# Gaps of 64 and 128 bytes ahead of the weight buffers of a two-layer encoder on one core

## The chip, the core and the metric

The kernel runs on one core of a Trainium2 chip. TensorE multiplies, VectorE, ScalarE and GpSimd work beside it on the same on-chip memory (SBUF, 128 partitions), DMA queues bring weights from HBM. The metric is the device time of one execution in microseconds. The kernel before took 1790.79 us (median of three runs, 1790.58 to 1791.91).

## The reference

The input is x with 512 tokens of 1024 features, in float32. There are two layers; each does

```python
x = x + 0.5 * swiglu(rms_norm(x, ffn1_norm[l]), ffn1_w_gate[l], ffn1_w_up[l], ffn1_w_down[l])
h = rms_norm(x, mix_norm[l])
p = h @ w_in[l]                       # latents of q and kv, rotary key, conv columns
attn = mla_group(...)                 # 8 heads, block-causal in chunks of 64
conv = conv_group(...)                # gate, causal depthwise conv of 31 taps, LayerNorm, silu
x = x + concatenate([attn, conv]) @ w_out[l]
x = x + 0.5 * swiglu(rms_norm(x, ffn2_norm[l]), ffn2_w_gate[l], ffn2_w_up[l], ffn2_w_down[l])
x = rms_norm(x, post_norm[l])
```

with `swiglu(x, g, u, d) = (silu(x @ g) * (x @ u)) @ d` and an inner width of 2816. Nearly all arithmetic is in the four feed-forward blocks.

## The kernel before

Features stand on the partitions and the 512 tokens along the free axis, so a tile of 128 features is 2048 bytes a partition. A product in float32 is made of three matmuls in a reduced float32 format (FR in the code): each operand is split into a high part, the operand rounded to FR, and a low part, what is left. `mm3` (lines 169 to 173) issues the three for one block of 128 x 128 weights: high weights with the high half of the moving operand (L170), the same weights with its low half (L171), low weights with its high half (L172). The moving operand has 512 columns, or 256 where a block works on half the tokens. `load_w` (lines 147 to 159) brings weights by a DMA of SyncE into a raw tile; ScalarE casts it to the high part (L151) and VectorE subtracts to the low part (L157). `split_into` (lines 257 to 263) does the same from tiles that are there already (L260, L262).

The feed-forward block of one layer (`ffn_body`) goes through the inner width in four chunks. The first pairs of columns are plain products. In the others, `pair` and `down` use a scheme with seven products in place of eight, on sums and differences of quarters of the weights and of x; most of these products have a moving operand of 256 columns. In some (`product_joined`, L389 and L390) the moving tile xj holds the high and the low half side by side: L389 multiplies all 512 columns by the high weights, L390 the first 256 by the low weights. The mixer (`mix_body`) has the same `mm3` for its projections; in `latent_k`, `queries` and `up_kv` the weights are the moving operand and the activations the stationary one.

The order of the work is the order in which the code issues it, with a scheduler of the framework behind it and some `issue_after` constraints that name an instruction by hand. Each engine works its own list and waits by semaphores.

The tiles lie in SBUF pool after pool, in the order in which the pools are opened, and inside a pool tag after tag, in the order of a tag's first use. The pools are: constants and x; the ring of 35 tiles of 2048 bytes (r), from which nearly all split activations come; 5 temporary tiles (t); the weights' pool with 3 raw buffers, 4 high (wh) and 4 low (wl) of 4096 bytes; a pool of small tiles; and then, by turns, the pool of a feed-forward block (fr raw quarters, xj and xs moving tiles, ls low weights that a DMA with addition makes) or that of the mixer (m and others). A pool that is larger by some bytes moves all that lies behind it.

What an address is for the change is the offset of a buffer's first byte in a partition. All large buffers have multiples of 512 bytes, so one offset modulo 512 holds for a whole tag. In the kernel before, ring, temporary, raw, wh and wl tiles are at 192, and fr, xj, xs, ls and m at 224.

Of the kernel before, what the change touches and what calls it, by code (L numbers as in the profile page):

```python
# [7 lines left out]
FP = mybir.dt.float32  # L8
FR = mybir.dt.float32r
# [6 lines left out]
P = 128  # L16
# [4 lines left out]
NT = S // P  # L21
H = 8
DN = 64
DR = 32
# [7 lines left out]
NF = F // P  # L32
EPS = 1e-6
WC = 1024
HS = S // 2
RING = 35
WIDE = 6
# [41 lines left out]
def encoder_kernel(ctx: ExitStack, tc: tile.TileContext, xT, consts, vecs, rgain, wgu1, wd1, wdq1,  # L79
# [6 lines left out]
    wpool = ctx.enter_context(tc.tile_pool(name="w", bufs=4))  # L86
    small = ctx.enter_context(tc.tile_pool(name="small", bufs=2))
# [3 lines left out]
    def nm(s):  # L91
        uid[0] += 1
        return f"{s}{uid[0]}"

    def slot(dt=FP, w=S):
        return ring.tile([P, w], dt, tag="r", name=nm("r"))
# [4 lines left out]
    def bank():  # L101
        return psum.tile([P, S], FP, tag="ps", name=nm("ps"))
# [10 lines left out]
    def tiny(tag, w, dt=FP):  # L113
        return small.tile([P, w], dt, tag=tag, name=nm(tag))

    V, A, G, T = nc.vector, nc.scalar, nc.gpsimd, nc.tensor

    x = cpool.tile([P, KD, S], FP, name="x")
# [28 lines left out]
    def load_w(src, w, kind=""):  # L147
        raw = wpool.tile([P, WC], FP, tag="raw", name=nm("raw"), bufs=3)
        nc.sync.dma_start(out=raw[:, :w], in_=src)
        hi = wpool.tile([P, WC], FR, tag="wh", name=nm("wh"))  # L150
        order["cast"] = A.copy(hi[:, :w], raw[:, :w]).ins  # L151
        lo = low()
        if kind == "sum":
            A.activation(lo[:, :w], raw[:, :w], AF.Copy, scale=-1.0)
            G.dma_start(out=lo[:, :w], in_=src, accum_op=ALU.add)
            return hi, lo
        (G if kind in POOLW.split() else V).tensor_tensor(lo[:, :w], raw[:, :w], hi[:, :w].bitcast(FP),  # L157
                                                          ALU.subtract)
        return hi, lo

    def low():
        return wpool.tile([P, WC], FR, tag="wl", name=nm("wl"))

# [5 lines left out]
    def mm3(o, lh, ll, rh, rl, first, last, free=False):  # L169
        T.matmul(o, lh, rh, start=first, stop=False, skip_group_check=free)  # L170
        T.matmul(o, lh, rl, start=False, stop=False, skip_group_check=free)  # L171
        order["mm"] = T.matmul(o, ll, rh, start=False, stop=last, skip_group_check=free).ins  # L172
        return order["mm"]
# [74 lines left out]
    def groups(srcs, rhs, ws=None):  # L248

        ws = ws or [load_w(src, WC) for src in srcs]  # L250
        os = [bank() for _ in srcs]
# [4 lines left out]

    def split_into(q, src, w=WC):

        hi = wpool.tile([P, WC], FR, tag="wh", name=nm("wh"))
        A.copy(hi[:, :w], src[:, :w])  # L260
        lo = low()
        order["lo"] = V.tensor_tensor(lo[:, :w], src[:, :w], hi[:, :w].bitcast(FP), ALU.subtract).ins  # L262
        return hi, lo
# [5 lines left out]
    def ffn_body(fpool, l, gx, norm, wgu, wd, wdq, gain, done, w0, halved):  # L269
# [52 lines left out]
        def operands(R):  # L322

            def joined(src):
                both = fpool.tile([P, 2, S], FR, tag="xj", name=nm("xj"), bufs=WIDE)
                A.copy(both[:, :, 0:HS], src)
                V.tensor_tensor(both[:, :, HS:S], src, both[:, :, 0:HS].bitcast(FP), ALU.subtract)
                return both
# [13 lines left out]
            for i in range(2):  # L342
                e, o = wide(quarter()), wide(quarter())
                for j in range(2):
                    for par, t in ((0, e), (1, o)):
                        m = 4 * i + 2 * j + par
                        V.scalar_tensor_tensor(t[:, j], x[:, m, :], gain[:, m:m + 1], R, ALU.mult, ALU.mult)
                        yield
                b11, b12, b21, b22 = (v[:, :, h * HS:(h + 1) * HS] for v in (e, o) for h in range(2))
                for n, src in (("b11", b11), ("b21", b21)):  # L350
# [21 lines left out]
        def product(o, w, n, start, stop):  # L372
            with tc.issue_after(order["pe"]):
                for gu in range(2):
                    for k in range(4):
                        hi, lo = X[n][k // 2]
                        t = slice(k % 2 * HS, (k % 2 + 1) * HS)
                        c = slice(gu * 512 + k * P, gu * 512 + (k + 1) * P)
                        last = mm3(o[:, gu * HS:(gu + 1) * HS], w[0][:, c], w[1][:, c], hi[:, t], lo[:, t],
                                   start and gu == 0 and k == 0, stop and k == 3, True)  # L380
            order["pe"] = last

        def product_joined(os, w, n, start):
            with tc.issue_after(order["pe"]):
                for gu, o in enumerate(os):
                    for k in range(4):
                        both = X[n][k // 2][:, k % 2]
                        c = slice(gu * 512 + k * P, gu * 512 + (k + 1) * P)
                        T.matmul(o, w[0][:, c], both, start=start and k == 0, stop=False, skip_group_check=True)  # L389
                        last = T.matmul(o[:, 0:HS], w[1][:, c], both[:, 0:HS], start=False, stop=k == 3,  # L390
                                        skip_group_check=True).ins
# [237 lines left out]
    def mix(l, gx, norm, done):  # L629
        with tc.tile_pool(name="k", bufs=4) as kpool:  # L630
            mix_body(kpool, l, gx, norm, done)

    def mix_body(kpool, l, gx, norm, done):
# [49 lines left out]
        cqT, ckT, pq, scqs, vs = [], [], [], [], []  # L683
        ssl, sspe = tiny("ssl", NT), tiny("sspe", NT)
        ckl = [slot().rearrange("p (t c) -> p t c", t=2) for _ in range(NT // 2)]
        cke = tiny("cke", NT * DR).rearrange("p (t d) -> p t d", t=NT)
        q = kpool.tile([P, NT, H, DQ], FP, tag="q", name=nm("q"), bufs=1)
        kn = kpool.tile([P, NT, H, DQ], FP, tag="kn", name=nm("kn"), bufs=1)
        cq, wkl_, sk, ckc, ratio = (tiny(n, NT) for n in ("cq", "wkl", "sk", "ckc", "ratio"))
# [346 lines left out]
    class Finish:  # L1036
# [54 lines left out]
        def __call__(self):  # L1091
# [4 lines left out]
            for t in range(NT):  # L1096
# [8 lines left out]
    st = Stats()  # L1105
    f = gained(0, "g1", gx, first_gain)
    f(0)
    w0 = [tuple(wpool.tile([P, WC], t, tag=tag, name=nm(tag), bufs=n)
                for t, tag, n in ((FP, "raw", 3), (FR, "wh", 4), (FR, "wl", 4))) for _ in range(2)]

    def half_w(q, gu):
        raw, hi, lo = (v[:, gu * 512:(gu + 1) * 512] for v in w0[q])
# [12 lines left out]
    w0 = [w[1:] for w in w0]  # L1125
# [172 lines left out]
```

## Time and profile before

| What | Value |
|---|---|
| median of three runs | 1790.79 us |
| profiled execution, its own time | 1792.67 us |
| its span, first to last instruction | 1790.6 us |
| TensorE busy, of the span | 99% |
| weight loads busy | 88% |
| VectorE, ScalarE, GpSimd busy | 83%, 61%, 21% |
| granted TensorE clock | 0.999 |
| mean HBM traffic | 127 GB/s |

The three runs lie within 0.1% of each other. The page calls TensorE's matmuls PE and its weight loads PEld; a weight load is a row of its own beside the matmuls. Matmuls are pipelined, so the busy time of a group is the union of durations that overlap, and the spacing of matmuls is read from the starts in the timeline. A row of the groups gives the line, the engine, the tile written and those read (buffer numbers left out), the shapes, the count, busy time, mean duration of one, and idle time before.

### The profile page before, as it was taken

The page shows a single profiled execution, that of the slowest core. Times are in us where ns is not written, and L with a number is a line of the kernel's source. Part 1 is how long each engine was busy: PE and PEld are TensorE (multiplying, and loading weights), DVE is VectorE, ACT ScalarE, POOL GpSimd, SP SyncE. Part 2 cuts the span into 40 slices and gives each one's busy share as a digit, 9 for nine tenths or more (in the row PEclk, how much of TensorE's full clock was granted, in tenths as well). Part 3 has the DMA queues.
Part 4 walks back from the last instruction along what each step waited for, and adds up shares of the span by engine and source line. Part 5 has one row for each costly group of instructions (what it writes and reads, how often), then busy time and mean ns, then how long its engine had stood idle before and what let it go on. Part 6 is the DMA issues. An engine that isn't in the chain of part 4 may idle for free.

```text
span 1790.6 us, 29441 instructions
## 1 busy us (share of the span) xinstructions
PE 1778.9 (99%) x11430; PEld 1580.5 (88%) x11430; DVE 1484.7 (83%) x2309; ACT 1094.0 (61%) x1699; POOL 383.4 (21%) x315
## 2 busy tenths in 40 slices
PE   9999999999999999999999999999999999999998
PEld 7899999888678899999888999998986788999997
DVE  7898988688965989898779989876989568989883
ACT  5575756457953575756645757564778435756564
POOL 1000010248822000000320000002576410000002
PEclk9999999999999999999999999999999999999999
DMA  4657574324203466665426575743261126575742
GB/s 169 163 139 182 136 178 116 116 78 125 75 24 100 124 165 158 157 157 135 124 65 166 124 193 126 190 111 120 72 159 29 59 72 175 127 186 130 185 115 74
DMA packets 71947, 228.28 MB, mean 127 GB/s; under 512 B 8448, under 2 KB 9600, under 8 KB 71808
## 3 DMA queue, kind: packets, MB, share of 16 engines
q1 hardware_dynamic: 55536, 171.87, 30.6%
q0 software_dynamic: 16128, 54.53, 18.0%
q8 instruction: 89, 1.46, 0.3%
q14 instruction: 50, 0.41, 0.1%
q10 hardware_dynamic: 144, 0.00, 0.0%
HBM read 222.19 MB, written 2.10 MB: 125 GB/s over the span
## 4 chain that ended last, share of the span: by engine, by line
PE 82%; DVE 3%; ACT 1%; DMA 0%; issue 0%; SPq 0%; ACTq 0%; DVEq 0%
PE ps L170 21%; PE ps L172 21%; PE ps L171 21%; PE ps L389 9%; PE ps L390 5%; PE ps L874 1%; PE ps L919 1%; PE ps L897 1%; DVE cv L970 1%; PE ps L912 0%; PE ps L676 0%; DVE mx L878 0%; PE ps L214 0%; DVE wl L262 0%; PE ps L233 0%; DMA r<-m 0%
## 5 line engine op out<-in xcount | busy, mean ns | idle before, releaser
L170 PE MATMUL ps<-r,wh 128*128 128x256 f32 (+1 forms) x2556 | 811.3, 321 | 2.6 <-ACT wh L1114 1.1
L171 PE MATMUL ps<-r,wh 128*128 128x256 f32 (+1 forms) x2556 | 812.9, 319 | 0.0
L172 PE MATMUL ps<-r,wl 128*128 128x256 f32 (+1 forms) x2364 | 755.5, 321 | 0.1
L170 PEld LDWEIGHTS ps<-r,wh 128*128 128x128 f32 x2556 | 483.7, 189 | 47.5 <-ACT wh L151 3.5
L171 PEld LDWEIGHTS ps<-r,wh 128*128 128x128 f32 x2556 | 484.5, 190 | 36.6 <-issue 1.9
L172 PEld LDWEIGHTS ps<-r,wl 128*128 128x128 f32 x2364 | 448.2, 190 | 34.6 <-DVE wl L157 0.4
L389 PE MATMUL ps<-xj,wh 128*128 128x512 f32 x864 | 303.8, 391 | 0.0
L151 ACT CAST wh<-raw 128x1024 fp32r<-128x1024 f32 (+3 forms) x148 | 132.5, 901 | 217.1 <-PE ps L171 124.8
L260 ACT CAST wh<-fr 128x1024 fp32r<-128x1024 f32 (+1 forms) x160 | 157.7, 986 | 105.9 <-DVE fr L426 45.8
L406 POOL DMA_DIRECT2D ls<-in_wgu x72 | 62.5, 868 | 734.7 <-ACT ls L405 525.4
L157 DVE TENSOR_TENSOR wl<-raw,wh 128x1024 fp32r<-128x1024 f32 (+3 forms) x132 | 141.9, 1083 | 89.6 <-ACT wh L151 88.4
L262 DVE TENSOR_TENSOR wl<-fr,wh 128x1024 fp32r<-128x1024 f32 (+1 forms) x160 | 181.9, 1137 | 20.4 <-ACT wh L260 20.4
L389 PEld LDWEIGHTS ps<-xj,wh 128*128 128x128 f32 x864 | 161.4, 188 | 30.1
L390 PE MATMUL ps<-xj,ls 128*128 128x256 f32 x576 | 161.3, 280 | 0.0
L976 POOL TENSOR_TENSOR y<-y,pr 128x495 f32<-128x495 f32 (+29 forms) x90 | 120.6, 1343 | 45.9 <-ACT pr L974 40.6
L260 ACT CAST wh<-raw 128x1024 fp32r<-128x1024 f32 (+1 forms) x100 | 98.1, 981 | 45.6 <-PE ps L171 24.9
L262 DVE TENSOR_TENSOR wl<-raw,wh 128x1024 fp32r<-128x1024 f32 (+1 forms) x100 | 113.3, 1133 | 14.2 <-ACT wh L260 13.8
L390 PEld LDWEIGHTS ps<-xj,ls 128*128 128x128 f32 x576 | 108.3, 188 | 0.0
L207 POOL TENSOR_TENSOR r<-r,t 128x512 f32<-128x512 f32 x45 | 75.4, 1684 | 132.4 <-ACT t L203 131.9
L405 ACT ACTIVATE ls<-fr 128x1024 fp32r<-128x1024 f32 (+1 forms) x56 | 56.1, 1002 | 75.6 <-PE ps L390 42.9
L970 DVE SCALAR_TENSOR_TENSOR cv<-m,vec,cv 128x511 f32<-128x511 f32 (+14 forms) x120 | 88.0, 733 | 4.6 <-ACT cv L966 3.0
L406 POOL DMA_DIRECT2D ls<-in_wdq x32 | 27.6, 863 | 262.6 <-ACT ls L405 262.6
(258 smaller groups left out, 2910.4 us busy)
## 6 DMA issues: line engine op xcount, KB each, us to landing
fr<-in_wgu SPq DMA_DIRECT2D x112, 512.0 KB, 4.2
ls<-in_wgu POOLq DMA_DIRECT2D x72, 512.0 KB, 6.4
raw<-in_wgu SPq DMA_DIRECT2D x62, 512.0 KB, 4.5
fr<-in_wdq SPq DMA_DIRECT2D x48, 384.0 KB, 4.8
ls<-in_wdq POOLq DMA_DIRECT2D x32, 384.0 KB, 4.8
raw<-in_wd SPq DMA_DIRECT2D x32, 384.0 KB, 3.2
raw<-in_wd SPq DMA_DIRECT2D x32, 256.0 KB, 2.7
raw<-in_wcv SPq DMA_DIRECT2D x16, 512.0 KB, 3.6
```

The source lines that it names most:

```text
L151: order["cast"] = A.copy(hi[:, :w], raw[:, :w]).ins
L157: (G if kind in POOLW.split() else V).tensor_tensor(lo[:, :w], raw[:, :w], hi[:, :w].bitcast(FP), ALU.subtract)
L170: T.matmul(o, lh, rh, start=first, stop=False, skip_group_check=free)
L171: T.matmul(o, lh, rl, start=False, stop=False, skip_group_check=free)
L172: order["mm"] = T.matmul(o, ll, rh, start=False, stop=last, skip_group_check=free).ins
L260: A.copy(hi[:, :w], src[:, :w])
L262: order["lo"] = V.tensor_tensor(lo[:, :w], src[:, :w], hi[:, :w].bitcast(FP), ALU.subtract).ins
L389: T.matmul(o, w[0][:, c], both, start=start and k == 0, stop=False, skip_group_check=True)
L390: last = T.matmul(o[:, 0:HS], w[1][:, c], both[:, 0:HS], start=False, stop=k == 3, skip_group_check=True).ins
L406: G.dma_start(out=lo[:, :n], in_=w, accum_op=ALU.add)
L970: V.scalar_tensor_tensor(acc[:, s:], u[c][:, :S - s], tap(k), acc[:, s:], ALU.mult, ALU.add)
L976: order["conv"] = G.tensor_tensor(ys[c][:, s:], ys[c][:, s:], pr[:, s:], ALU.add).ins
```

## The change

The program of each engine is word for word the same list with the same waits: no instruction is added, taken away or moved, only addresses are others. Four edits do it:

- The weights' pool gets a tile of 16 floats (64 bytes) between the raw and the high buffers, and one of 32 floats (128 bytes) between the high and the low ones. Nothing reads or writes them.
- The small pool gets a tile of 96 floats (384 bytes) that nothing uses, ahead of its other tiles.
- `cke`, the rotary part of the keys, has one buffer of 512 bytes in place of two.

So wh moves by 64 bytes and wl by 192, and all behind the small pool by 64 + 128 + 384 - 512 = 64. Offsets modulo 512, and the distance from the moving operand to the weights:

| buffers | before | after |
|---|---|---|
| ring r, temporary t, raw | 192 | 192 |
| high weights wh | 192 | 256 |
| low weights wl | 192 | 384 |
| fr, xj, xs, ls, m | 224 | 288 |

| moving, weights | distance before | after |
|---|---|---|
| r, wh | 0 | +64 |
| r, wl | 0 | +192 |
| r, ls | +32 | +96 |
| xj or xs or m, wh | -32 | -32 |
| xj or xs or m, wl | -32 | +96 |
| xj, ls | 0 | 0 |

```diff
+GAP = 96
...
+    small.tile([P, GAP], FP, tag="gap", name="gap", bufs=1)
     V, A, G, T = nc.vector, nc.scalar, nc.gpsimd, nc.tensor
...
-        cke = tiny("cke", NT * DR).rearrange("p (t d) -> p t d", t=NT)
+        cke = small.tile([P, NT, DR], FP, tag="cke", name=nm("cke"), bufs=1)
...
-    w0 = [tuple(wpool.tile([P, WC], t, tag=tag, name=nm(tag), bufs=n)
-                for t, tag, n in ((FP, "raw", 3), (FR, "wh", 4), (FR, "wl", 4))) for _ in range(2)]
+    w0 = [tuple(wpool.tile([P, w], t, tag=tag, name=nm(tag), bufs=n) for t, tag, n, w in (
+        (FP, "raw", 3, WC), (FP, "gap0", 1, 16), (FR, "wh", 4, WC), (FP, "gap1", 1, 32), (FR, "wl", 4, WC)))[::2]
+        for _ in range(2)]
```

## The prediction

> **What bounds the kernel now.** I read the page first (busy times, then the chain that ended last), then the waits of TensorE, then the groups of matmuls with their shapes kept apart, and last the timeline of TensorE in five short stretches, because the change moves no instruction and only the spacing of matmuls can answer it.
>
> ```profile
> PE 1778.9 (99%) x11430; PEld 1580.5 (88%) x11430; DVE 1484.7 (83%) x2309; ACT 1094.0 (61%) x1699; POOL 383.4 (21%) x315
> ...
> PE 82%; DVE 3%; ACT 1%; DMA 0%; issue 0%; SPq 0%; ACTq 0%; DVEq 0%
> ...
> core 0: 1790.6 us, clock 0.999
> ...
> PE ps L170 <- ACT wh L1114: 1.1, 1, 1.1
> ```
>
> TensorE is busy all the time, its longest wait for anybody in the whole run is 1.1 us, its clock is granted in full, and no other engine has more than 3% of the chain. So the time is the number of matmuls times the distance from one matmul's start to the next one's. The groups give the numbers (the line, then tiles written and read, moving shape, count, busy time and mean duration; a duration overlaps the next matmul's, so it is not the spacing):
>
> ```profile
> L170 PE MATMUL ps<-r,wh 128*128 128x256 f32 x1704 | 482.8, 283 | 0.6
> L171 PE MATMUL ps<-r,wh 128*128 128x256 f32 x1704 | 482.2, 283 | 0.0
> L172 PE MATMUL ps<-r,wl 128*128 128x256 f32 x1512 | 427.7, 283 | 0.1
> L171 PE MATMUL ps<-r,wh 128*128 128x512 f32 x852 | 331.1, 390 | 0.0
> L170 PE MATMUL ps<-r,wh 128*128 128x512 f32 x852 | 328.4, 395 | 2.0 <-ACT wh L1114 1.1 <-ACT wh L151 0.8
> L172 PE MATMUL ps<-r,wl 128*128 128x512 f32 x852 | 328.3, 390 | 0.0
> ...
> L390 PE MATMUL ps<-xj,wl 128*128 128x256 f32 x288 | 78.2, 281 | 0.0
> L172 PE MATMUL ps<-r,ls 128*128 128x256 f32 x192 | 54.1, 282 | 0.0
> ...
> L172 PE MATMUL ps<-xs,wl 128*128 128x256 f32 x144 | 40.6, 282 | 0.0
> ```
>
> The first six rows are the matmuls whose moving operand is a ring tile and whose weights are wh or wl, the pairs of the title: 3 groups of 256 columns, 1704 + 1704 + 1512 = 4920, and 3 of 512 columns, 3 x 852 = 2556; 7476 of 11430. The spacing is read from the timeline (start, duration), between the first and the last row of a stretch without a break:
>
> ```profile
> 301.36 0.28 PE L170 MATMUL ps<-r,wh 128*128 128x256 f32 x1
> ...
> 301.71 0.28 PE L170 MATMUL ps<-r,wh 128*128 128x256 f32 x1
> ...
> 303.15 0.28 PE L170 MATMUL ps<-r,wh 128*128 128x256 f32 x1
> ...
> 303.15 0.19 PEld L171 LDWEIGHTS ps<-r,wh 128*128 128x128 f32 x1
> ...
> 516.97 0.39 PE L170 MATMUL ps<-r,wh 128*128 128x512 f32 x1
> ...
> 518.33 0.39 PE L170 MATMUL ps<-r,wh 128*128 128x512 f32 x1
> ...
> 545.08 0.39 PE L170 MATMUL ps<-r,wh 128*128 128x512 f32 x1
> ...
> 546.46 0.39 PE L170 MATMUL ps<-r,wh 128*128 128x512 f32 x1
> ```
>
> From 301.71 to 303.15 are 12 matmuls, 120.0 ns each; from 516.97 to 518.33 are 6 of 512 columns, 226.7 ns each. The 256 columns more cost 106.7 ns, so each matmul, of either width, carries 13.3 ns beyond its columns. The weight load of the next matmul begins with the running one (both at 303.15), so two streams read SBUF together, and this is what an offset between their buffers could touch. Neither rate is there at once. After other work the 256-wide matmuls run quicker first (301.36 to 301.71: 3 in 0.35 us, 117 ns) and then settle at 120; the 512-wide run slower first (545.08 to 546.46: 6 in 1.38 us, 230 ns) and then settle at 226.7. The settled state is a loss for the narrow ones and a gain for the wide ones.
>
> **The change, part by part.** No engine's order or waits change, so no DMA, queue or semaphore is passed. What changes is 64 or 192 bytes between a ring tile's offset and the weights'. In the kernel before, ring, wh and wl all start at 192 bytes modulo 512, and the pool tiles (xj, xs, m, ls) at 224.
>
> Does an offset matter at all? Three other distances stand in the trace. First, 32 bytes, with pool tiles as moving operand and wh and wl as weights:
>
> ```profile
> 293.57 0.28 PE L170 MATMUL ps<-xs,wh 128*128 128x256 f32 x1
> ...
> 294.28 0.28 PE L170 MATMUL ps<-r,wh 128*128 128x256 f32 x1
> ...
> 530.57 0.40 PE L170 MATMUL ps<-m,wh 128*128 128x512 f32 x1
> ...
> 531.74 0.40 PE L170 MATMUL ps<-r,wh 128*128 128x512 f32 x1
> ```
>
> Six matmuls of xs take 0.71 us, 118.3 ns each and 1.7 below the settled 120. Five of m take 1.17 us, 234 ns each and 7.3 above the settled 226.7. Second, the key latents, where wh and wl are the moving operand, 288 columns, and start 0, 128 and 256 bytes from the ring tile, 12 matmuls each:
>
> ```profile
> 388.12 0.29 PE L170 MATMUL ps<-wh,r 128*128 128x288 f32 x1
> ...
> 389.69 0.29 PE L170 MATMUL ps<-wh,r 128*128 128x288 f32 x1
> ...
> 391.29 0.29 PE L170 MATMUL ps<-wh,r 128*128 128x288 f32 x1
> ...
> 392.87 0.29 PE L170 MATMUL ps<-wh,r 128*128 128x288 f32 x1
> ```
>
> They take 1.57, 1.60 and 1.58 us: 130.8, 133.3 and 131.7 ns. Third, the joined products, where low weights at the moving tile's own offset (ls) stand against low weights 32 bytes away (wl), with 512- and 256-wide matmuls in turn:
>
> ```profile
> 311.27 0.39 PE L389 MATMUL ps<-xj,wh 128*128 128x512 f32 x1
> ...
> 312.30 0.39 PE L389 MATMUL ps<-xj,wh 128*128 128x512 f32 x1
> ...
> 304.58 0.39 PE L389 MATMUL ps<-xj,wh 128*128 128x512 f32 x1
> ...
> 306.66 0.39 PE L389 MATMUL ps<-xj,wh 128*128 128x512 f32 x1
> ```
>
> Three pairs with ls take 1.03 us, 343 ns a pair; six with wl take 2.08 us, 347 ns. So an offset is worth a few ns a matmul, with either sign.
>
> Term one, the 4920 narrow matmuls. No row has a distance of 64 or 192 bytes. Ends: 113.3 ns, half of the 13.3 away, and 122.5, the 2.5 ns that 128 bytes cost the latents. I take 118.3, that of xs, the only row of this width and this way round with wh and wl away from the moving tile: 4920 x -1.7 = -8.4 us. Ends: -33 and +12 us.
>
> Term two, the 2556 wide ones. Ends: 220, half of the 13.3 away (-17 us), and 234, the rate of m (+18.7 us). I take no change: the ring tiles come back to 226.7 after every disturbance, and the new distances are multiples of 64 bytes as those of the latents are, where the cost of 0.9 to 2.5 ns lies nearer to nothing than that of m.
>
> The rest. 288 + 192 + 144 = 624 matmuls of xj with wl, r with ls and xs with wl get a distance that is 64 or 128 bytes another; at the 4 ns between the two kinds of pair that is 2.5 us to either side, and I take nothing. The pairs of xj and xs with wh and of xj with ls keep their distance, since both sides move by 64. VectorE and ScalarE read and write the moved buffers too, but
>
> ```profile
> L262 DVE TENSOR_TENSOR wl<-fr,wh 128x1024 fp32r<-128x1024 f32 x112 | 136.4, 1218 | 20.4 <-ACT wh L260 20.4
> L262 DVE TENSOR_TENSOR wl<-raw,wh 128x1024 fp32r<-128x1024 f32 x68 | 82.8, 1218 | 10.8 <-ACT wh L260 10.8
> ...
> L822 DVE TENSOR_TENSOR kn<-cke,scp x8: 411/415/422, 436.2 to 1326.0; 128x256 f32<-128x256 f32 x8
> ```
>
> the same subtraction takes 1218 ns from fr, 32 bytes off, and from raw, at wh's own offset: nothing, and TensorE covers it; were that cover gone, the unchanged 1218 would still add nothing. The single cke buffer makes the second layer's first copy wait for the first layer's last read; its eight last reads, four a layer, run from 436.2 to 1326.0, over 800 us from one layer to the other, so no wait.
>
> The sum is -8.4 us. The profiled execution took 1792.67 us, its span 1790.6 and 2.1 around it, and would take 1784.3; the median of the runs shown is 1790.79, 1.9 less, and would be 1782.4.
>
> A rule speaks against all this. The Trainium skill, SBUF — State Buffer, section Who interferes with whom, gives TensorE two independent read ports, one for the moving operand and one for weight loads, and lets it wait for nobody. By it the sum is 0 and the time 1790.8; the trace disagrees in part, with 118.3 and 234 ns where only offsets differ from the 120 and 226.7.
>
> **The rivals.** *Nothing moves.* The settled rates come from the width alone, and steps of 64 bytes leave them. For it: 120.0 and 226.7 have the same 13.3 ns, and the latents stay within 2.5 ns over 256 bytes. Against it: xs and m. Time 1790.8, within 3.6 us.
>
> *Slower: the wide matmuls lose their settled state.* Place: the plain products, the down projections and the mixer's projections, 2556 matmuls. At the 230 of the unsettled stretch they cost 3.3 x 2556 = +8.4 us, at the 234 of m +18.7: 1799 to 1809 if the narrow ones stay at 120. If these gain their 8.4, it is 1791 to 1801, and it decides from 4.7 ns on ((8.4 + 3.6) / 2556); alone, from 1.4 ns on. For it: m, and all 128-byte distances of the latents cost something. Against it: m also starts in the middle of a 64-byte step, which no ring tile does.
>
> *Much faster: the 13.3 ns is a collision of the two streams that the gaps end.* Half of it gone from all 7476 is 6.7 x 7476 = -50 us, 1741. For it: the weight load starts with the matmul. Against it: no distance in these rows goes below 117 for long. The Trainium skill, TensorE: Matmul & The Clock Gate, section Back-to-back issue gap, states N / 2.4 + 2.5 ns for a warm matmul by itself, an estimate of 109 and 216 ns here; by it 10.8 ns of the 13.3 would be at stake and the time 1710. The trace has 120 and 226.7.
>
> **How the numbers follow.** Forecast, narrow matmuls quicker and wide ones kept: 0.40, own range 1776 to 1787. Nothing moves: 0.19. Slower: 0.35, as m is the plainest row against me. Much faster: 0.06. A measurement of this kernel tells about 0.2%, 3.6 us, from no change, so faster has 0.46, same 0.19, slower 0.35. The range goes up to 1808, all but the worst of the slower case, and down to 1766, halfway from term one's value to its lower end and a little more, which leaves out the much faster case and the tails of the others.
>
> **What would show it.** In the profile after, the timeline in the same products: 256-wide ring matmuls 118 ns apart or less, 512-wide ones 226.7. If the 512-wide stand at 230 to 234, the slower rival is right; if both stand at 120.0 and 226.7, nothing moved; if either stands near 113 or 220, the collision was real. Waits of TensorE should stay at about 1 us; if they grow instead, a quicker TensorE has caught up with the weight splits on ScalarE and VectorE (83% busy), and part of the gain is lost there. My forecast is wrong if the distance of 64 or 192 bytes has a state of its own that none of these rows shows.

## The result, and the profile after

The kernel after takes 1782.63 us (median of five runs, 1781.53 to 1783.28); the kernel before, run beside it, took 1790.79 (1790.33 to 1791.96). The ratio is 0.9951, with a 95% interval of 0.9939 to 0.9962. The profiled execution of after took 1781.53 us with a span of 1779.8, 10.8 us less than the span before; by the medians the gain is 8.2 us, since the profiled execution of before lay 1.9 us above its median and that of after 1.1 below. The time is the one forecast to 0.3 us. The way to it is not: both kinds of ring matmul changed their spacing, in opposite directions.

The page of the kernel after, with TensorE's busy row and the chain by engine; then the span and clock; then two rows of TensorE's waits:

```profile
PE 1768.6 (99%) x11430; PEld 1558.0 (88%) x11430; DVE 1486.0 (83%) x2309; ACT 1094.9 (62%) x1699; POOL 383.3 (22%) x315
...
PE 91%; DVE 5%; ACT 2%; issue 1%; DMA 1%; SPq 0%; ACTq 0%; DVEq 0%
```

```profile
core 0: 1779.8 us, clock 0.999
```

```profile
PE ps L133 <- DVE ones L129: 1.1, 1, 1.1
...
PE ps L173 <- DVE r L180: 0.4, 1, 0.4
```

What bounds the kernel is as before: TensorE is busy for 99% of the span at the full clock, and waits for nobody for more than 1.1 us. TensorE is busy 10.3 us less and the span is 10.8 us shorter, so the gain lies between the starts of its matmuls. The groups of the kernel after, shapes kept apart (line, tiles, moving shape, count, busy time, mean duration; the lines of `mm3` are now L172 to L174):

```profile
L172 PE MATMUL ps<-r,wh 128*128 128x256 f32 x1704 | 477.4, 280 | 1.0
L173 PE MATMUL ps<-r,wh 128*128 128x256 f32 x1704 | 474.3, 278 | 0.8 <-DVE r L180 0.4
L174 PE MATMUL ps<-r,wl 128*128 128x256 f32 x1512 | 420.4, 278 | 0.0
L174 PE MATMUL ps<-r,wl 128*128 128x512 f32 x852 | 334.0, 396 | 0.0
L173 PE MATMUL ps<-r,wh 128*128 128x512 f32 x852 | 333.4, 392 | 0.0
L172 PE MATMUL ps<-r,wh 128*128 128x512 f32 x852 | 331.3, 399 | 0.7 <-ACT wh L1117 0.6
```

Against the rows shown of before the three narrow groups fall from 482.8, 482.2 and 427.7 to 477.4, 474.3 and 420.4 us of busy time, and the three wide ones rise from 328.4, 331.1 and 328.3 to 331.3, 333.4 and 334.0. That is the sign of each; the size is read from the starts. In the timeline of the kernel after, first the places that answer to 301.71 to 303.15 and to 545.08 to 546.46 of before, then two longer stretches without a break, of 42 narrow and of 96 wide matmuls:

```profile
297.12 0.28 PE L172 MATMUL ps<-r,wh 128*128 128x256 f32 x1
298.48 0.28 PE L172 MATMUL ps<-r,wh 128*128 128x256 f32 x1
...
541.05 0.39 PE L172 MATMUL ps<-r,wh 128*128 128x512 f32 x1
542.45 0.39 PE L172 MATMUL ps<-r,wh 128*128 128x512 f32 x1
...
161.69 0.28 PE L172 MATMUL ps<-r,wh 128*128 128x256 f32 x1
166.34 0.28 PE L174 MATMUL ps<-r,wl 128*128 128x256 f32 x1
...
417.38 0.40 PE L172 MATMUL ps<-r,wh 128*128 128x512 f32 x1
439.41 0.40 PE L174 MATMUL ps<-r,wl 128*128 128x512 f32 x1
```

and the first and last rows of the same two longer stretches in the kernel before:

```profile
163.29 0.28 PE L170 MATMUL ps<-r,wh 128*128 128x256 f32 x1
168.20 0.28 PE L172 MATMUL ps<-r,wl 128*128 128x256 f32 x1
...
420.88 0.39 PE L170 MATMUL ps<-r,wh 128*128 128x512 f32 x1
442.42 0.39 PE L172 MATMUL ps<-r,wl 128*128 128x512 f32 x1
```

Narrow: 12 spacings in 1.36 us are 113.3 ns, where before had 120.0; over the stretch of 41 spacings, 4.65 us are 113.4 ns where before had 4.91, 119.8. Wide: 6 spacings in 1.40 us are 233 ns, and 95 in 22.03 us are 231.9 ns, where before had 21.54, 226.7. The wide ring matmuls never come back to 226.7 in the kernel after.

Not all products are settled, so for the narrow ones the difference of the means over all spacings is smaller than that of the settled rates. The table below is worked out from the starts of all TensorE matmuls of each trace, put in program order; spacings more than 35 ns above the time of the columns (N / 2.4 ns for N columns, from the 106.7 ns that 256 columns cost) are taken out of the means, and for all matmuls that read wh, wl or ls their excess over N / 2.4 + 13.3 is added up as "breaks". A joined pair is the mean of xj on 512 columns where ls follows, plus that of xj on 256 columns where wh follows; it stands for the 576 pairs with ls, and the 288 with wl are 1 to 4 ns longer. The kernels below the second row are those of the experiments.

| kernel | narrow ring, ns | wide ring, ns | joined pair, ns | breaks, us | span, us |
|---|---|---|---|---|---|
| before | 119.6 | 227.2 | 346.8 | 16.8 | 1790.6 |
| after | 115.0 | 231.8 | 345.0 | 19.3 | 1779.8 |
| both64 | 115.3 | 233.3 | 345.2 | 22.5 | 1787.9 |
| low192 | 117.8 | 230.9 | 349.2 | 17.1 | 1792.1 |
| sq_none | 119.6 | 227.2 | 350.2 | 27.3 | 1802.9 |
| sq_narrow | 115.1 | 227.2 | 345.0 | 34.3 | 1784.4 |
| sq_wide | 119.6 | 231.9 | 350.1 | 27.2 | 1814.1 |
| sq_both | 115.1 | 231.9 | 345.0 | 36.8 | 1797.2 |
| best0 | 119.5 | 227.2 | 350.0 | 16.7 | 1794.8 |
| best64 | 115.2 | 227.2 | 345.2 | 22.7 | 1773.0 |

From before to after: 4920 narrow matmuls at 4.6 ns less are -22.6 us, 2556 wide ones at 4.6 ns more +11.8, 576 joined pairs with ls at 1.8 ns less and 288 with wl at 0.8 less -1.3, breaks +2.5. Together -9.6 us, of the span's -10.8. Of the rest, the 1121 matmuls that read none of wh, wl and ls (attention, convolution, sums) took 2.0 us less in this trace, and several small groups together 0.6 more. The 2.0 us are probably of the one profiled execution of before, which lay 1.9 us above its median; that was not shown.

### The profile page after: what moved, and what is told of

Its sections match the earlier page's. It is cut to its first block, busy times and chain, and to the rows that moved or that the text cites. A ratio compares the mean times of both kernels' runs of the same rounds, so it can differ in the third digit from the quotient of the medians.

```text
span 1779.8 us, 29441 instructions
## 1 busy us (share of the span) xinstructions
PE 1768.6 (99%) x11430; PEld 1558.0 (88%) x11430; DVE 1486.0 (83%) x2309; ACT 1094.9 (62%) x1699; POOL 383.3 (22%) x315
## 3 DMA queue, kind: packets, MB, share of 16 engines
q0 software_dynamic: 16128, 54.53, 18.3%
## 4 chain that ended last, share of the span: by engine, by line
PE 91%; DVE 5%; ACT 2%; issue 1%; DMA 1%; SPq 0%; ACTq 0%; DVEq 0%
PE ps L172 24%; PE ps L174 24%; PE ps L173 23%; PE ps L391 11%; PE ps L392 6%; DVE cv L972 1%; PE ps L921 1%; DVE mx L880 1%; PE ps L899 1%; DVE wl L264 1%; PE ps L876 0%; PE ps L678 0%; PE ps L216 0%; PE ps L914 0%; DVE r L902 0%
## 5 line engine op out<-in xcount | busy, mean ns | idle before, releaser
L172 PE MATMUL ps<-r,wh 128*128 128x256 f32 (+1 forms) x2556 | 808.8, 320 | 1.7 <-ACT wh L1117 0.6
L174 PE MATMUL ps<-r,wl 128*128 128x256 f32 (+1 forms) x2364 | 753.9, 321 | 0.0
L172 PEld LDWEIGHTS ps<-r,wh 128*128 128x128 f32 x2556 | 480.6, 188 | 51.0 <-issue 3.7
L174 PEld LDWEIGHTS ps<-r,wl 128*128 128x128 f32 x2364 | 444.1, 188 | 38.5 <-DVE wl L159 0.7
L264 DVE TENSOR_TENSOR wl<-raw,wh 128x1024 fp32r<-128x1024 f32 (+1 forms) x100 | 113.8, 1138 | 11.8 <-ACT wh L262 11.2
```

## The experiments

**Three probes with only matmuls.** They measure what a distance costs outside the encoder, where ScalarE, VectorE and DMA are idle while TensorE works. The core of the first, with the moving tiles at one offset and the weights dh and dl bytes further, each from 0 to 448 in steps of 64; at each setting two narrow products, two wide and two joined follow one another:

```python
def weights(dh, dl):
    return wt[:, dh // 4:dh // 4 + 1024], wt[:, 1152 + dl // 4:1152 + dl // 4 + 1024]
...
for dh, dl in GRID:
    for m in MODES:
        done[m](*weights(dh, dl))
```

> The encoder is left out: this kernel runs only matmuls of float32r tiles, in the three forms of the encoder (256 columns in threes, 512 columns in threes, joined pairs of 512 and 256 columns), with the moving tiles at offset 192 as the ring has and the high and low weights at every pair of distances of 0, 64, ... 448 bytes from them; its output is zeros. Theory (the distance between the moving operand's offset and the offset of the weights that are loaded meanwhile sets the spacing, TensorE alone): at distances 0 and 0 the settled spacing is 120.0 ns for 256 columns and 226.7 for 512, at 64 and 192 it is 113.3 and about 232, as in the two encoders; between the 64 pairs the narrow spacing varies by 5 ns or more. Rival (the other engines' reads and writes at the new offsets, or the pool tiles that moved with the gaps, make the difference): without other engines all 64 pairs have the same spacing within 1 ns, for either width.

The timeline of this probe, first and last row of 24 spacings, taken over the second of two equal products of a setting: narrow and wide at (0, 0), then narrow and wide at (64, 192):

```profile
16.51 0.28 PE L47 MATMUL b<-mv,wt 128*128 128x256 f32 x1
...
19.38 0.28 PE L47 MATMUL b<-mv,wt 128*128 128x256 f32 x1
...
24.74 0.39 PE L57 MATMUL b<-mv,wt 128*128 128x512 f32 x1
...
30.18 0.39 PE L57 MATMUL b<-mv,wt 128*128 128x512 f32 x1
...
262.29 0.28 PE L47 MATMUL b<-mv,wt 128*128 128x256 f32 x1
...
265.01 0.28 PE L47 MATMUL b<-mv,wt 128*128 128x256 f32 x1
...
270.45 0.40 PE L57 MATMUL b<-mv,wt 128*128 128x512 f32 x1
...
276.01 0.39 PE L57 MATMUL b<-mv,wt 128*128 128x512 f32 x1
```

2.87, 5.44, 2.72 and 5.56 us over 24 spacings: 119.6 and 226.7 ns at the distances of the kernel before, 113.3 and 231.7 at those of the kernel after. These are the settled spacings of the two encoders, so no other engine is needed for the effect. The spacings of the last product of each setting, narrow / wide, in ns:

| dh \ dl | 0 | 64 | 128 | 192 |
|---|---|---|---|---|
| 0 | 119.7 / 226.7 | 117.8 / 231.1 | 118.9 / 231.1 | 117.6 / 231.1 |
| 64 | 122.2 / 231.1 | 113.3 / 233.3 | 118.2 / 231.1 | 113.3 / 231.7 |
| 128 | 118.3 / 233.3 | 117.8 / 230.0 | 118.8 / 232.7 | 116.7 / 233.4 |
| 192 | 117.8 / 228.9 | 113.3 / 233.3 | 115.5 / 233.5 | 117.8 / 228.9 |

The wide matmul is best at (0, 0), the narrow one at (64, 64), (64, 192) and (192, 64); no setting has both. Larger distances add nothing new: with 256 bytes more on one side or on both, the wide table repeats within 0.8 ns in 16 of 16 places, the narrow one in 15 of 16. The exception is (64, 0): 122.2 ns where the setting before it was (0, 192), 117.8 where it was (64, 192), all modulo 256.

The Trainium skill, SBUF — State Buffer, section Who interferes with whom, gives the moving operand and the weight loads independent read ports. If that meant that their places do not matter, all 16 places would be alike; they range from 113.3 to 122.2 and from 226.7 to 233.5 ns.

The second probe takes odd multiples of 32 bytes:

```diff
-STEP = 64
-GRID = [(a * STEP, b * STEP) for a in range(8) for b in range(8)]
+STEP = 32
+GRID = [(a * STEP, b * STEP) for a in range(8) for b in range(8) if a % 2 or b % 2]
```

> The encoder is left out, as in the first probe; only distances of which one or both are odd multiples of 32 bytes, from 0 to 224. Theory (spacing is a function of the two distances modulo 256): each pair settles at a value of its own between 113 and 122 ns (256 columns) and 226 and 234 (512); at -32 and -32, which is 224 and 224, the narrow one stands near the 118 of the xs products and the wide one near the 234 of the m products of the kernel before. Rival (only multiples of 64 bytes count, 32 is rounded away): each pair equals its neighbour in the first probe.

In none of its 48 settings does either width settle at its best: the narrow ones lie between 116.8 and 124.4 ns and the wide ones between 228.9 and 235.6. The pool tiles xj, xs and m, an odd multiple of 32 bytes from wh and wl in both kernels, are in this class; at (224, 224), the distances of xs and m to wh and wl before, it has 117.8 and 233.3 ns, near the 118.3 and 234 of the prediction's rows.

The third moves everything, moving tiles and weights, by 32 bytes, and takes all 64 settings:

```diff
-STEP = 64
+STEP = 32
...
-SHIFT = 0
+SHIFT = 32
```

> The encoder is left out; all 64 pairs of distances of 0, 32, ... 224 bytes, with moving tiles and weights together 32 bytes further on (moving tiles at offset 224, as the pool tiles of the kernel before). Theory (only the distance between the two counts): the table of the first probe comes out again, 120 and 226.7 at 0 and 0, 113.3 at 64 and 64. Rival (the place of a tile itself within 64 bytes counts too): other values, such as no settled 226.7 at 0 and 0.

The wide table is that of the first two probes within 0.8 ns in 62 of 64 places, with 226.7 at (0, 0) alone. So for the wide matmuls the distance counts and not the address. The narrow table agrees in 55 of 64, and (64, 192) is 113.3 again; but (64, 64) is 117.8 in place of 113.3, and (192, 64) 118.9. What differs is not spread over the table. In 32 places, those with dh an odd multiple of 32, the setting that ran just before is the same in both probes, and there both widths agree in 32 of 32, with everything moved by 32 bytes. All places that differ, 9 narrow and 2 wide, are among the other 32, where another setting ran before. So a product can settle at more than one rate at the same distance, and what ran before it probably decides; that was not varied by itself.

**Other distances in the encoder.** Two kernels with the change's layout and another gap. One puts both weights 64 bytes off:

```diff
-        (FP, "raw", 3, WC), (FP, "gap0", 1, 16), (FR, "wh", 4, WC), (FP, "gap1", 1, 32), (FR, "wl", 4, WC)))[::2]
+        (FP, "raw", 3, WC), (FP, "gap0", 1, 16), (FR, "wh", 4, WC), (FR, "wl", 4, WC), (FP, "gap1", 1, 32)))
...
+    w0 = [(t[0], t[2], t[3]) for t in w0]
```

> The 128-byte gap stands behind the low weights in place of ahead of them: high and low weights are both 64 bytes from the ring, all else is as in the changed kernel. Theory, by the probe's table: 256-wide ring matmuls 113.3 ns as in the changed kernel, 512-wide 233.3 in place of 231.7, so 2556 x 1.6 = 4 us slower than the changed kernel, about 1786.5. Rival (it is the gap between high and low weights that helps, not their distance from the ring): the gain of 8 us goes, 1791.

1789.51 us (1787.25 to 1791.17), 0.9992 of before (0.9982 to 1.0001). That is nearer to the rival's 1791 than to the 1786.5 expected, but the spacings decide against the rival: the narrow matmuls are nearly as quick as in the kernel after (115.3 for 115.0 ns, 1.5 us). It is 7 us worse than that kernel because the wide ones take 1.5 ns more, as in the probe (233.3 for 231.7), 3.8 us, and the breaks add 3.2, which were not part of the expectation.

The other moves only the low weights, by 192:

```diff
-        (FP, "raw", 3, WC), (FP, "gap0", 1, 16), (FR, "wh", 4, WC), (FP, "gap1", 1, 32), (FR, "wl", 4, WC)))[::2]
+        (FP, "raw", 3, WC), (FR, "wh", 4, WC), (FP, "gap0", 1, 48), (FR, "wl", 4, WC)))
...
+    w0 = [(t[0], t[1], t[3]) for t in w0]
```

> High weights stay at the ring's offset, low ones are 192 bytes from it, pools as in the changed kernel. Theory, by the probe's table: 256-wide ring matmuls 117.6 ns in place of 120 (4920 x -2.4 = -12 us), 512-wide 231.1 in place of 226.7 (2556 x 4.4 = +11 us), so within 3 us of the kernel before, about 1790. Rival (either gap alone gives its part of the gain): near 1786.

1793.68 us (1792.79 to 1795.44), 1.0018 of before (1.0008 to 1.0028). Narrow 1.8 ns less (-8.9 us), wide 3.7 more (+9.5), joined pairs 2.4 and, with wl, 3.3 more (+2.3): +2.9 by these terms, +3.1 by the medians (before had 1790.58 beside it). Here, too, a gain and a loss cancel.

**Narrow and wide apart.** This is the experiment on the forecast's step: the two kinds of product get their distances independently. Each weight buffer is 64 bytes longer, and `load_w` (all wide products, and 72 narrow matmuls) takes another view of it than `split_into` and `summed` (the other 4848 narrow ones and the joined). There was no room for the longer buffers, so small tiles stand in the spaces between them; for that each buffer has a tag of its own, and the framework then lists some instructions of VectorE and ScalarE in another order, and in 17 joined products some of TensorE's. The four kernels share that order and differ in four numbers (the remarks behind # are added here):

```diff
+WP = WC + 16
+AT_WIDE, AT_NARROW = (0, 16), (0, 16)      # sq_none; (16, 0) puts a kind at 64 and 192
...
-        hi = wpool.tile([P, WC], FR, tag="wh", name=nm("wh"))      # load_w
+        hi = high(AT_WIDE)
...
-        hi = wpool.tile([P, WC], FR, tag="wh", name=nm("wh"))      # split_into, summed
+        hi = high(AT_NARROW)
...
+    def high(at):
+        return kept("wh", 4, [P, WP], FR)[:, at[0]:at[0] + WC]
```

> One of four kernels with the same program, in which only the offsets differ at which the weights stand in their buffers; every buffer of weights has 64 bytes more, small tiles stand in the spaces between the buffers, and the products on 512 columns can have their weights at another offset than those on 256 columns. Here all ring products have weights at distances 0 and 0, as in the kernel before, while the other pools' tiles stand to the ring as in the kernel after. Theory (the two kinds of ring matmul, each by its own distance): 1790.8, with 3 us either way for the other order that the vector and scalar engines have in these four. Rival (the moved pools behind the weights make the gain, not the weights' distance from the ring): 1782.6, the same as the other three within 2 us.

> Of the four: weights of the products on 256 columns (and of the joined ones) at distances 64 and 192 as in the kernel after, weights of the products on 512 columns at 0 and 0 as in the kernel before. Theory: 4848 narrow ring matmuls at 4.5 ns less (119.6 to 115.1 mean in the traces of before and after) are 21.8 us, and the wide ones stay at 226.7: 1769, within 4 us, with wide groups as before and narrow groups as after. Rival (one kind of product leaves a state in which the other starts, so that the two effects don't add): 1779 to 1790, with narrow groups back near 120 or wide ones near 231. Rival (the pools): 1782.6.

> Of the four, the opposite: weights of the products on 512 columns at 64 and 192, those of the narrow and joined products at 0 and 0. Theory: 2556 wide ring matmuls at 4.6 ns more (227 to 231.7 mean) are 11.8 us on top of the kernel before: 1802.5, within 4 us. Rival (the two effects don't add): 1790 to 1797. Rival (the pools): 1782.6.

> Of the four: all ring products at 64 and 192, so that every distance of a moving tile from its weights is that of the kernel after. Theory: 1782.6, within 3 us for the other order on the vector and scalar engines, and the sum of the two steps: none minus narrow, plus wide minus none, comes to none minus both within 2 us. Rival (the two effects don't add): the four differ from that sum by more than 4 us.

| us | wide at 0, 0 | wide at 64, 192 |
|---|---|---|
| narrow at 0, 0 | sq_none 1804.82 (1804.52 to 1805.15) | sq_wide 1815.46 (1814.67 to 1815.88) |
| narrow at 64, 192 | sq_narrow 1786.49 (1785.24 to 1789.21) | sq_both 1798.04 (1796.21 to 1798.97) |

Against before the ratios are 1.0081 (1.0066 to 1.0096), 1.0139 (1.0122 to 1.0156), 0.9979 (0.9969 to 0.9988) and 1.0042 (1.0027 to 1.0057). Moving the narrow products alone takes 18.3 us away, moving the wide ones alone adds 10.6, and the sum of both steps, 1797.1, is 0.9 from the kernel with both. The effects add. The first step is more than the narrow ring matmuls, since the joined products move with them: between the traces of sq_none and sq_narrow the ring matmuls give 21.8 us (4848 x 4.5) and the joined pairs 4.2, and breaks take 7.0 back. The rival by which the moved pools make the gain falls, since the four have the same pools and span 29 us. The ring groups of sq_narrow, of which only the narrow ones differ from before:

```profile
L206 PE MATMUL ps<-r,wh 128*128 128x256 f32 x1704 | 475.4, 279 | 9.6 <-DVE r L213 9.6
L205 PE MATMUL ps<-r,wh 128*128 128x256 f32 x1704 | 475.1, 279 | 0.5 <-DVE x L531 0.4
...
L206 PE MATMUL ps<-r,wh 128*128 128x512 f32 x852 | 331.1, 390 | 0.0
L205 PE MATMUL ps<-r,wh 128*128 128x512 f32 x852 | 328.5, 396 | 0.8 <-ACT wh L183 0.8
L207 PE MATMUL ps<-r,wl 128*128 128x512 f32 x852 | 328.4, 390 | 0.0
```

The level was missed by 13 to 17 us in all four: 1804.8 where 1790.8 was expected for sq_none. The time of sq_narrow lies in the range of its rival (1779 to 1790), but its groups are not the rival's, by which the narrow ones would be back near 120 or the wide ones near 231. In the groups of sq_none the narrow ones wait:

```profile
L206 PE MATMUL ps<-r,wh 128*128 128x256 f32 x1704 | 482.3, 283 | 8.7 <-DVE r L213 8.7
...
L207 PE MATMUL ps<-r,wl 128*128 128x256 f32 x1512 | 428.8, 284 | 3.8 <-DVE wl L297 3.8
```

12.5 us in which TensorE waits for VectorE, which now has the low parts later in its list; in before these two groups had 0.1. The breaks grow by 10.5 us; the joined pairs (350.2 for 346.8 ns) are another 2.7. The ring matmuls have the spacings of before, so it was not their distances.

**The same without the new order.** To keep one tag and still have the room, the constant tiles of ones become a column that is read 128 times over, and each weight buffer gets 4352 bytes. Every engine then has the order of before and after, and 4352 bytes are 17 times 256. best0 is the control, best64 the version that the experiments point to:

```diff
-GAP = 96
+GAP = 16
+WP = WC + 64
+AT_WIDE, AT_NARROW = 0, 16                 # best64; best0 has 0, 0
...
-    onesm = cpool.tile([P, P], FP, name="onesm")
-    V.memset(onesm, 1.0 / CW)
+    V.memset(column[:, 2:3], 1.0 / CW)
+    onesm = column[:, 2:3].to_broadcast([P, P])
...
+    def high(at):
+        return wpool.tile([P, WP], FR, tag="wh", name=nm("wh"))[:, at:at + WC]
```

> The control of the next run, with the order of before and after on every engine: buffers of weights of 4352 bytes, the constant tiles of ones shrunk to a column that is read 128 times over to make room for them, the tiles of the attention and feed-forward pools 96 bytes off the ring's as in the kernel after, and all ring products at distances 0 and 0. If the 14 us that the four kernels above had in common come from their order on the vector and scalar engines: 1790.6 plus at most 2.5 us for the joined pairs (41.9 for 36.9 cycles over the columns in the trace of sq_none), that is 1790 to 1794. If the gain of the kernel after came from the moved pools: 1783. If the 14 us come from the wider buffers themselves: 1800 to 1806.

> The same with the weights of the products on 256 columns (and of the joined ones) 64 bytes into their buffers: narrow ring products at distances 64 and 64, wide ones at 0 and 0. Theory: the narrow matmuls give 4848 times 4.3 ns (120 less the 115.3 to 115.7 of both64), 21 us, the wide ones nothing, and some 3 to 6 us of that are lost to waits for the vector and scalar engines, as in both64 (22.5 us of intervals that are more than 35 ns above the columns' time, for 16.8 before): 1772, within 4 us, which would be 8 to 14 us under the kernel after. Rival (waits take most of the gain, since the other engines are then late): 1780 to 1784, with over 10 us of waits on TensorE. Rival (narrow and wide don't add): 1783 or more with few waits.

best0 takes 1793.91 us (1793.31 to 1796.84), 1.0021 of before (1.0012 to 1.0030), 10.9 less than sq_none with the same distances and spacings: its breaks are 10.6 us fewer. So that much came with the tags and the order; where the small tiles and constants lie differs too, and was not tested apart. The other 3 us are the joined pairs (350.0 for 346.8 ns). best64 takes 1775.95 (1774.78 to 1777.89), 0.9923 of before (0.9909 to 0.9937), the fastest of all, and 6.7 us under the kernel after (before had 1790.41 beside it, and 1790.79 beside after). The 1772 expected was met within its 4 us by a hair, but 8 to 14 us under the kernel after were expected too, and that was missed. From its groups, its timeline, and the longest waits of the matmuls (PE) and of the weight loads (PEld) for another engine:

```profile
L177 PE MATMUL ps<-r,wh 128*128 128x256 f32 x1704 | 478.2, 281 | 1.2
L178 PE MATMUL ps<-r,wh 128*128 128x256 f32 x1704 | 475.0, 279 | 0.7
L179 PE MATMUL ps<-r,wl 128*128 128x256 f32 x1512 | 421.1, 278 | 0.1
L178 PE MATMUL ps<-r,wh 128*128 128x512 f32 x852 | 331.0, 390 | 0.0
L177 PE MATMUL ps<-r,wh 128*128 128x512 f32 x852 | 328.7, 396 | 1.3 <-ACT wh L155 0.6 <-ACT wh L1120 0.6
L179 PE MATMUL ps<-r,wl 128*128 128x512 f32 x852 | 328.3, 390 | 0.0
```

```profile
161.27 0.28 PE L177 MATMUL ps<-r,wh 128*128 128x256 f32 x1
165.92 0.28 PE L179 MATMUL ps<-r,wl 128*128 128x256 f32 x1
...
250.23 0.28 PE L177 MATMUL ps<-r,wh 128*128 128x256 f32 x1
255.06 0.28 PE L179 MATMUL ps<-r,wl 128*128 128x256 f32 x1
...
416.41 0.39 PE L177 MATMUL ps<-r,wh 128*128 128x512 f32 x1
437.94 0.39 PE L179 MATMUL ps<-r,wl 128*128 128x512 f32 x1
```

```profile
PE ps L881 <- ACT r L889: 1.0, 2, 0.5
...
PEld ps L177 <- ACT t L406: 5.4, 24, 0.2
```

The narrow groups are near those of after, the wide ones within 0.3 us of before. Of the two narrow stretches of 41 spacings, one settles at 113.4 ns (4.65 us) and one at 117.8 (4.83 us), at the same distances modulo 256; the wide stretch has 226.6 (21.53 us over 95). The gap of 18 us between best64 and best0 is -20.8 from the narrow matmuls (4848 x 4.3), -3.5 from the joined pairs and +6.0 of breaks. (The spans lie 21.8 apart: the profiled execution of best0 was 2.9 us above its median, and the 1121 other matmuls took 2.8 us more in it than in that of best64.) So of the 24.3 us that the matmuls gave, a quarter went into breaks. A part of them can be seen: 24 weight loads behind joined products wait for ScalarE's copy of a bank (L406), a row that best0 does not have, and 8 wait 2.4 in place of 1.4 us for low parts of VectorE (L185). The breaks behind these are 2.6 us of the 6.0: there the quicker TensorE has caught up with ScalarE and VectorE. For the other 3.4 the profile names nobody.

Which rate do the narrow matmuls settle at? In each trace, take all stretches of 24 or more narrow ring matmuls without a break, and of each the mean of the last 12 spacings. At (64, 192) it is near 113.3 ns in 98 of 98 stretches of the kernel after and in 105 of 105 of sq_both. At (64, 64) there are two rates: in both64, where all buffers have one offset modulo 512, 66 stretches are near 113.3 and 32 near 117.8, and in best64 70 and 27 (one is at 120). By the means 64 and 192 are worth little more (115.0 and 115.1 ns against 115.3 and 115.2, about 1 us over 4848 matmuls); narrow products at 64 and 192 with the order of best64 were not run.

**Which weights does a moving tile meet?** The last probe tries to tell a matmul's own weights from those that are loaded while it runs, with two moving tiles s bytes apart (shortened, remarks added):

```python
if k % 2 == 0:
    T.matmul(o[:, 0:n], wt[:, a + c:a + c + P], first, ...)     # A, c1 from tile 1
else:
    T.matmul(o[:, 0:n], wt[:, b + c:b + c + P], second, ...)    # B, c2 from tile 2
```

> Only matmuls, nothing of the encoder (the output is zeros). Two moving tiles and two weights in turn: tile 1 with weights A, tile 2 with weights B, 48 times on 256 columns and 48 times on 512. A stands c1 bytes from tile 1, B c2 bytes from tile 2, and tile 2 stands 0, 64 or 128 bytes (s) further than tile 1 modulo 256, so that while tile 1 streams the weights to be loaded are those of tile 2, c2 + s from it, and while tile 2 streams they are c1 - s from it. c1 and c2 go through 0, 64, 128 and 192. Theory 'next' (the moving tile meets the weights that are loaded meanwhile, those of the next matmul): the table for s is that for s = 0 with c1 - s and c2 + s in place of c1 and c2; so with s = 64 the pair (64, 192) has what (0, 0) has for s = 0, near 120 and 226.7, and (0, 0) has what (192, 64) has, near 113 on 256 columns and 229 to 233 on 512. Rival 'own' (a matmul's tile against its own weights): the three tables are alike, (0, 0) near 120 and 226.7 in each.

| s, narrow / wide in ns | (0, 0) | (64, 64) | (64, 192) | (192, 64) |
|---|---|---|---|---|
| 0 | 120.0 / 226.7 | 113.3 / 233.3 | 113.3 / 231.2 | 113.3 / 231.1 |
| 64 | 116.7 / 231.7 | 118.9 / 230.0 | 120.0 / 231.7 | 118.4 / 230.0 |
| 128 | 116.6 / 228.3 | 116.7 / 230.0 | 116.7 / 231.1 | 116.7 / 231.0 |

The rival "own" falls, since the tables differ: (0, 0) has neither 120 nor 226.7 once the tiles are apart. The theory "next" has two hits for s = 64, 120.0 narrow at (64, 192) and 231.7 wide at (0, 0), and two misses, 231.7 wide at (64, 192) in place of 226.7 and 116.7 narrow at (0, 0) in place of 113. Over all 32 settings with s = 64 or 128 and both widths, "next" comes within 1 ns in 16 of 64 values and "own" in 21, so neither holds. No setting with s = 64 or 128 reaches 113.3, and one reaches 226.7: (64, 0) at s = 64, where both weights stand at the offset of the second tile. So more than one distance takes part, and which pairs of reads meet stays open.

## Why the prediction came out right

The time was right, 1782.63 for 1782.4, by two wrong terms that cancel: that it came within 0.3 us is luck. By the signs that the prediction named itself, the mechanism was another: 512-wide ring matmuls at 230 to 234 were the sign of the rival "slower", and they stand at 231.8; its last line, a distance of 64 or 192 bytes with a state of its own that no row of before shows, is what the probes found.

- *What bounds the kernel.* Right: the order, the waits and the clock stayed, and the gain lies in the spacing of matmuls.
- *Term one, the narrow matmuls, 118.3 ns and -8.4 us.* Right in sign, mis-sized. They settle at 113.3, the end that was kept for "half of the 13.3 away"; with the unsettled starts of products the mean went from 119.6 to 115.0, -22.6 us. The step that failed is taking the rate from xs: that row has the weights 32 bytes off, and the second probe shows no narrow rate under 116.8 at any odd multiple of 32. A distance of 64 has a state that no row of before had.
- *Term two, the wide matmuls, nothing.* Wrong. They went from 227.2 to 231.8 ns, +11.8 us. The reason given, that ring tiles come back to 226.7 after every disturbance, was an observation at distance 0 alone; the first probe has 226.7 there and in none of the other 15 places. The other reason, the 0.9 to 2.5 ns of the latents, came from 288 columns; at 512 columns the 15 places cost 2.2 to 6.8 ns. The rival "slower" had this mechanism, its place and its price (+8.4 to +18.7) right. What it lacked was the size of the narrow gain: with the 22.6 measured, the loss would have had to exceed 8.8 ns a wide matmul to cancel it, not the 3.3 that the 8.4 gave.
- *The rival "much faster".* Half right: the settled narrow matmuls lost half of their 13.3 ns, the wide ones none of it. That the 13.3 ns are a collision of the two reads was not shown.
- *The rest, nothing within 2.5 us.* The joined pairs gave 1.3 us, though the distances of the 576 with ls did not change, and why is open; the breaks took 2.5. VectorE's busy time went from 1484.7 to 1486.0, so the moved buffers cost it nothing that counts.
- *The rival "nothing moves".* Against the traces: four kernels that differ in offsets alone lie 29 us apart.

sq_narrow and sq_wide show the two terms apart, 18.3 us (with the joined pairs, and less the breaks) and 10.6, and best64 keeps the first without the second.

## What to carry to other kernels

In a kernel whose time is the spacing of matmuls with a weight load each, the distance between the moving tiles and the weights, modulo 256 bytes, matters: it was worth 0.8% here, and the best setting depends on the number of columns: here 0 for both weights on 512 columns, and 64 for the high and 192 for the low ones on 256. When products of two widths share buffers, give each its own offset within the buffer rather than one gap for all. A net change that comes out as forecast says little about its terms; the spacing of each kind of matmul has to be read before the reason is believed.

## What was not expected of the hardware

- The effect has a period of 256 bytes in the distance (16 of 16 wide places, 15 of 16 narrow ones, the exception behind another setting). It is the same at an absolute offset 32 bytes on wherever the setting before was the same (32 of 32 places), and it needs no other engine: the probes have it with TensorE alone.
- At one distance there can be more than one settled rate: at (64, 64) 113.3 and 117.8 ns in both64, in best64 and between two probes, while (64, 192) had 113.3 alone. Which of them a product takes was not settled, so a small test of a product alone may not show the rate that it has in a kernel.
- The version with a tag of its own for each weight buffer took 10.9 us more (sq_none against best0), more than the whole change gave: VectorE's order was another, and TensorE waited 12.5 us for low parts of weights and activations.
